# Query and key projections of a two-layer encoder, made with tokens instead of channels on the partitions, in one stream with the Fourier input

## The chip, the cores and the metric

One core of a Trainium2 chip runs the whole program in one launch. The metric is the device time of an execution in microseconds (us). The kernel before took 2951.58 us (median of 3 runs, 2950.15 to 2954.19). TensorE is written PE in the views, its weight loads PEld, VectorE DVE, ScalarE ACT, GpSimd POOL, and SyncE, which issues most DMAs, SP.

## What is computed

Two layers on a residual stream x of 256 tokens by 2048 channels, all in float32. Each has a token mixer, a cross-attention into 256 memory tokens and a gated MLP with a width-3 convolution. The change touches the start of the token mixer:

```python
h = rms_norm(x, mix_pre_g[l])
proj = h @ w_in                       # 2048 x (2048 q + 512 k + 512 v + 1024 fourier)
q = apply_axial_rope(rms_norm(q, q_norm_g), cos, sin)   # 16 heads of 128
k = apply_axial_rope(rms_norm(k, k_norm_g), cos, sin)   # 4 heads of 128
a = blocked_gqa(q, k, v) @ w_attn_o   # softmax attention, 4 q heads to a k head
f = fourier_mix(uf) @ w_four_o        # Re(2-D DFT over positions and channels)
g = sigmoid(h @ w_gate + b_gate)
y = (g[:D] * a + g[D:] * f) @ w_mix_o
```

The rotation takes, in each half of a head, 32 channels x1 and 32 channels x2 to (x1 cos - x2 sin, x2 cos + x1 sin).

## The kernel before

Every float32 product is made of three products of a reduced type: each operand is split into a high and a low part, and high x high, high x low and low x high are summed in PSUM. The activations are split once (A, with channels on the partitions, the high parts of 256 tokens beside their low parts). The weights are split on the fly: a DMA of 512 KB brings 128x1024 floats (w), ScalarE casts them (whi, L133), VectorE subtracts (wlo, L134). Two such pieces are a `Unit` of 1 MB. The pools w, whi and wlo have four buffers each, so a unit is loaded and split while the one before it is multiplied.

There are two ways to multiply. *Weight-stationary* (`ws_chunk`, `block`, L148 to L170): a unit holds the weights of one head's 128 channels for all 16 blocks of input channels; per block one matmul has whi as its stationary operand and streams high and low parts of A (512 columns, L151), a second has wlo and streams the high part (256 columns, L152). The result has channels on the partitions; its two halves are added (`merge`). *Activation-stationary* (`ko_as`, `mm_rows`, L296 to L303): the stationary operand is a 128-token block of A, and 512 columns of weights stream; per input block and token block there are three matmuls of 512 columns. The result has tokens on the partitions. A unit then holds 4 of the 16 input blocks of 512 output columns, and takes 24 matmuls.

A token mixer before the change runs in this order. v, and then the Fourier input in two groups of 512 columns, are made activation-stationary (`ko_as`; the groups are called as). The 20 heads of k and q follow in pairs (`heads`, L608 to L642), weight-stationary: ScalarE squares into hsq, moves 32-partition pieces for the rotation (L600), VectorE rotates with tables over channels (L601 to L606), GpSimd adds squares (L620), and four tiny matmuls per pair sum the squares over partitions (ps_h, L631). The norm of k is spread over the partitions with more small matmuls (ps_kn, L252) and multiplied in. The norm of q is applied later, as the scale of the softmax. Then comes the Fourier stage (`tokens`, `channels`; the matmuls dft and dftx), in which the tiny matmuls of the last pair still stand, and then attention over heads, with the gate projections (g), the Fourier output and the attention output (a) in between.

A tile scheduler sets the order on each engine, and puts in the semaphore waits. Each engine works its own queue in order. At the start of layer 0 SP also loads x once more with tokens on the partitions (X, L558, 2 MB), whose squares (L294) give the norm of the input.

Of the kernel before, what the change touches and what calls it, by code (L numbers as in the profile page):

```python
# [16 lines left out]
P = 128  # L17
# [18 lines left out]
O_BG, O_CW0, O_CW1, O_CW2, O_CB, O_QG, O_KG, NPAR = 112, 144, 232, 320, 408, 496, 497, 498  # L36
# [7 lines left out]
def encoder(ctx: ExitStack, tc: tile.TileContext, t, out):  # L44
# [21 lines left out]
    sides = cp.tile([P, 2], F32, tag="sides", name="sides")  # L66
    nc.vector.memset(sides, 0.0)
    for a in range(2):
        nc.vector.memset(sides[a * 64 : (a + 1) * 64, a : a + 1], 1.0)

# [9 lines left out]
    cos_t = con[:, C_COS : C_COS + T]  # L80
    sin_t = con[:, C_SIN : C_SIN + T]
# [332 lines left out]
    def boundary(y, steps, gains, A, cols, fill=()):  # L414
# [100 lines left out]

    def gains_of(p_, g0):
        return [p_[:, g0 + k : g0 + k + 1] for k in range(KT)]
# [29 lines left out]
    for k in range(KT):  # L547
# [3 lines left out]
        if k == 1:  # L551
            next(feed)
            next(feed)
        if k % 2:
            next(feed)
# [9 lines left out]
    for l in range(L):  # L565
# [5 lines left out]
        k_r = kug[:, 0:4]  # L571
# [3 lines left out]
        def token_major(pss, dst):  # L575
            for j in range(2):
                nc.scalar.activation(dst[:, j], pss[j], AF.Copy, scale=pre.t[:, j : j + 1])

        pss = []
        feed = ko_as(t["w_vu"][l, 1], A, pss)  # L580
        for _ in range(4):
# [6 lines left out]
        for j in range(2):  # L588
            scaled_split(pss_v[j], pre.t[:, j : j + 1], [v[:, j] for v in v_hl])
        run(feed)  # L590
        token_major(pss, u_s[:, :, 0:512])
        pss = []
        run(ko_as(t["w_vu"][l, 2], A, pss))
        token_major(pss, u_s[:, :, 512:1024])

        def rope(raw, g, dst):

            x2 = tmp2("x2")
            for a, b in ((0, 32), (32, 0), (64, 96), (96, 64)):
                nc.scalar.activation(x2[a : a + 32], raw[b : b + 32], AF.Copy, scale=par[b : b + 32, g : g + 1])  # L600
            nc.vector.scalar_tensor_tensor(  # L601
                out=dst, in0=raw, scalar=par[:, g : g + 1], in1=cos_t[:, None, :].to_broadcast([P, 2, T]),
                op0=ALU.mult, op1=ALU.mult,
            )
            nc.vector.tensor_mul(x2, x2, sin_t[:, None, :].to_broadcast([P, 2, T]))
            nc.vector.tensor_add(dst, dst, x2)  # L606

        def heads(w, i, n, g, dst):  # L608

            raw = tmp2("raw")  # L610
            for j in range(2):
                merge(ws_chunk(w[j], A, KT, name="qk"), raw[:, j])
                if j == 0:
                    yield

            sq = tmp2("hsq")
            for a in range(2):
                for b in range(2):
                    nc.scalar.activation(sq[64 * a : 64 * a + 64, b], raw[64 * b : 64 * b + 64, a], AF.Square)
            nc.gpsimd.tensor_add(sq[:, 0], sq[:, 0], sq[:, 1])  # L620
            if dst is None:

                dst = tmp2("q")
                rope(raw, g, dst)
                split(dst, O[:, i : i + 2].rearrange("p h s n -> p s h n"))
            else:
                rope(raw, g, dst)
            yield
            ps = psum_pv("ps_h")
            for j in range(2):  # L630
                nc.tensor.matmul(  # L631
# [611 lines left out]
```

## Time and profile before

| | |
|---|---|
| time, median of 3 runs | 2951.58 us |
| time of the profiled execution | 2949.64 us |
| its span, first to last instruction | 2947.9 us |
| PE busy | 2917.1 us (99%) |
| VectorE, ScalarE, GpSimd busy | 2057.7, 1646.4, 29.6 us |
| DMA | 562.63 MB, mean 191 GB/s |
| granted clock of TensorE | 0.999 of full speed |
| k and q projection, layer 0 | 75.76 to 194.56 us |
| k and q projection, layer 1 | 1545.60 to 1664.75 us |

The first line of the page gives busy time by engine; matmuls are pipelined, so how long a stream of matmuls takes is read from the starts of its instructions in the timeline and not from their durations. The chain of waits (part 4 of the page) tells which engine the end waited for.

### The profile page before, as it was taken

What the parts mean: (1) busy time and instruction counts of PE and PEld (TensorE: products, weight loads), DVE (VectorE), ACT (ScalarE), POOL (GpSimd) and SP (SyncE); (2) the same over time, 40 slices, a digit from 0 to 9 for tenths busy, and PEclk for the clock granted to TensorE, in tenths of its full rate; (3) what the DMA queues carried; (4) which work ended last, traced back from release to release, by engine and by line L of the source; (5) the groups of instructions that cost most, each with busy time, mean ns of one, the idle gap of its engine ahead of it and who ended that gap; (6) DMA issues with size and microseconds to landing.
All of it is one profiled execution on the core that took longest, in us unless ns stands there. A gap on an engine that the chain in (4) does not pass through costs nothing.

```text
span 2947.9 us, 39901 instructions
## 1 busy us (share of the span) xinstructions
PE 2917.1 (99%) x14844; PEld 2464.5 (84%) x14844; DVE 2057.7 (70%) x2963; ACT 1646.4 (56%) x2517; POOL 29.6 (1%) x40
## 2 busy tenths in 40 slices
PE   9999999999999999999999999999999999999998
PEld 7888888887888888888878888888878888888887
DVE  5678766666775767767756786776667757677676
ACT  5776545556554545545547764445565545455454
POOL 0000000000000000000000000000000000000000
PEclk9999999999999999999999999999999999999999
DMA  7554766765456565565645446667554565655655
GB/s 282 166 158 144 233 225 224 226 189 180 163 185 196 186 185 193 183 196 186 214 162 168 143 154 219 220 220 226 189 178 163 182 199 186 187 192 180 199 186 164
DMA packets 162756, 562.63 MB, mean 191 GB/s; under 512 B 18432, under 2 KB 18688, under 8 KB 162432
## 3 DMA queue, kind: packets, MB, share of 16 engines
q1 hardware_dynamic: 160992, 555.61, 58.5%
q0 software_dynamic: 1280, 4.20, 0.4%
q8 instruction: 116, 1.90, 0.3%
q14 instruction: 80, 0.66, 0.1%
q10 hardware_dynamic: 288, 0.27, 0.0%
HBM read 555.81 MB, written 4.19 MB: 190 GB/s over the span
## 4 chain that ended last, share of the span: by engine, by line
PE 92%; DVE 3%; DMA 2%; ACT 2%; issue 1%; SPq 0%; POOL 0%; DVEq 0%; ACTq 0%; POOLq 0%
PE up L151 21%; PE up L152 11%; PE y L303 7%; PE y L302 7%; PE y L301 7%; PE qk L151 4%; PE g L303 4%; PE g L301 4%; PE g L302 4%; PE qk L152 2%; PE a L303 2%; PE a L302 2%; PE a L301 2%; PE as L211 1%; PE as L212 1%; PE as L210 1%
## 5 line engine op out<-in xcount | busy, mean ns | idle before, releaser
L134 DVE TENSOR_TENSOR wlo<-w,whi 128x1024 fp32r<-128x1024 f32 (+1 forms) x989 | 1184.4, 1201 | 667.5 <-ACT whi L133 665.1
L133 ACT CAST whi<-w 128x1024 fp32r<-128x1024 f32 (+1 forms) x989 | 1019.4, 1034 | 1022.2 <-PE up L151 388.1
L151 PE MATMUL up<-A_ff,whi 128*128 128x512 f32 x2688 | 946.2, 397 | 0.0
L152 PE MATMUL up<-A_ff,wlo 128*128 128x256 f32 x2688 | 754.4, 281 | 0.0
L151 PEld LDWEIGHTS up<-A_ff,whi 128*128 128x128 f32 x2688 | 504.6, 188 | 122.4
L152 PEld LDWEIGHTS up<-A_ff,wlo 128*128 128x128 f32 x2688 | 507.8, 189 | 0.3
L302 PE MATMUL y<-wlo,G 128*128 128x512 f32 x704 | 274.1, 389 | 0.8 <-DVE wlo L134 0.8
L301 PE MATMUL y<-whi,G 128*128 128x512 f32 x704 | 274.1, 389 | 0.2 <-ACT whi L133 0.2
L303 PE MATMUL y<-whi,G 128*128 128x512 f32 x704 | 274.0, 389 | 0.0
L151 PE MATMUL qk<-A_mix,whi 128*128 128x512 f32 x640 | 227.2, 398 | 0.0
L303 PE MATMUL g<-whi,A_mix 128*128 128x512 f32 x512 | 201.7, 394 | 0.0
L301 PE MATMUL g<-whi,A_mix 128*128 128x512 f32 x512 | 201.2, 393 | 0.4 <-DVE work L763 0.4
L302 PE MATMUL g<-wlo,A_mix 128*128 128x512 f32 x512 | 200.2, 391 | 0.0
L152 PE MATMUL qk<-A_mix,wlo 128*128 128x256 f32 x640 | 179.3, 280 | 0.0
L302 PEld LDWEIGHTS y<-wlo,G 128*128 128x128 f32 x704 | 132.2, 188 | 28.4 <-DVE wlo L134 1.1
L301 PEld LDWEIGHTS y<-whi,G 128*128 128x128 f32 x704 | 132.1, 188 | 28.0 <-ACT whi L133 0.7
L303 PEld LDWEIGHTS y<-whi,G 128*128 128x128 f32 x704 | 132.1, 188 | 27.6
L151 PEld LDWEIGHTS qk<-A_mix,whi 128*128 128x128 f32 x640 | 120.2, 188 | 27.5
L152 PEld LDWEIGHTS qk<-A_mix,wlo 128*128 128x128 f32 x640 | 120.8, 189 | 0.1
L303 PEld LDWEIGHTS g<-whi,A_mix 128*128 128x128 f32 x512 | 96.2, 188 | 19.2
L301 PEld LDWEIGHTS g<-whi,A_mix 128*128 128x128 f32 x512 | 96.3, 188 | 19.0 <-ACT whi L133 0.8
L302 PEld LDWEIGHTS g<-wlo,A_mix 128*128 128x128 f32 x512 | 96.3, 188 | 18.7
(264 smaller groups left out, 4040.9 us busy)
## 6 DMA issues: line engine op xcount, KB each, us to landing
w<-in_w_up SPq DMA_DIRECT2D x336, 512.0 KB, 3.9
w<-in_w_dn SPq DMA_DIRECT2D x160, 512.0 KB, 3.7
w<-in_w_g SPq DMA_DIRECT2D x128, 512.0 KB, 4.2
w<-in_w_qk SPq DMA_DIRECT2D x80, 512.0 KB, 5.0
w<-in_w_ao SPq DMA_DIRECT2D x64, 512.0 KB, 4.8
w<-in_w_mo SPq DMA_DIRECT2D x64, 512.0 KB, 4.1
w<-in_w_vu SPq DMA_DIRECT2D x47, 512.0 KB, 4.8
w<-in_w_fo SPq DMA_DIRECT2D x32, 512.0 KB, 4.6
```

Source lines behind the costliest of these rows:

```text
L133: nc.scalar.copy(hi[:, :m], w[:, :m])
L134: nc.vector.tensor_sub(lo[:, :m], w[:, :m], hi[:, :m].bitcast(F32))
L151: nc.tensor.matmul(ps, hi, a, start=first, stop=False, skip_group_check=True)
L152: nc.tensor.matmul(ps[:, :T], lo, a[:, 0:T], start=False, stop=last, skip_group_check=True)
L210: nc.tensor.matmul(pss[j], ah, hi, start=kt == 0, stop=False)
L211: nc.tensor.matmul(pss[j], ah, lo, start=False, stop=False)
L212: nc.tensor.matmul(pss[j], al, hi, start=False, stop=kt == KT - 1)
L301: nc.tensor.matmul(ps, ah, hi, start=first, stop=False)
L302: nc.tensor.matmul(ps, ah, lo, start=False, stop=False)
L303: nc.tensor.matmul(ps, al, hi, start=False, stop=last)
```

## The change

- k and q are no longer made weight-stationary. `projected`, which made the gates, is moved up and makes them activation-stationary: five groups of 512 columns (4 heads each), k first, four units a group, 24 matmuls a unit. The two Fourier groups follow in the same stream (`in_columns`, `stream`). The weights lie in DRAM in the other layout, in the same amount.
- The first unit of that stream is prepared earlier: in layer 0 before the last blocks of x are used, in layer 1 in the boundary ahead of the squares of x.
- The norms are summed along the free dimension: for each token block j and head, ScalarE squares 128 columns of PSUM with an accumulated sum (8 per group).
- The rotation reads PSUM on VectorE: one multiplication of 128x512 by a table, two of 128x256 by the other (the halves exchanged by the access pattern), one addition. The gains are multiplied into the tables once per layer (`rotation`, four multiplications of 128x256, behind a broadcast load of 256 KB).
- The result (tokens on partitions) is turned by four transposes per token block and group on TensorE (rt), then split into high and low parts by ScalarE and VectorE, as q and k were before.
- The steps of this work are strewn into the stream by `between`, one per input block.
- Gone: the partition moves, the squares of half heads, GpSimd's additions, ps_h, ps_kn and `merge` of k and q.

```diff
@@ boundary
+        if then is not None:
+            then()
@@ start of layer 0
+        if k == KT - 1:
+            todo, later = in_columns(0)
+            todo[0].make()
@@ new functions
+    def stream(items, between):
+        for i, item in enumerate(items):
+            if i + 1 < len(items):
+                items[i + 1].make()
+            for _ in item.use():
+                between(i)
+                yield
+    def in_columns(l):
+        later = []
+        todo = []
+        for n in range(5):
+            todo += projected(t["w_qk"][l, n], A, "qk", lambda j, ps, row, n=n: later.append((n, j, ps)))
+        for n in range(2):
+            todo += projected(t["w_vu"][l, 1 + n], A, "u", lambda j, ps, row, n=n: later.append((5 + n, j, ps)))
+        return todo, later
@@ the layer
-        pss = []
-        feed = ko_as(t["w_vu"][l, 1], A, pss)
...
+        def rotated(n, j, ps):
...
+            def begin():
+                for h in range(4):
+                    nc.scalar.activation(
+                        unread[:, :P], ps[:, h * P : (h + 1) * P], AF.Square, accum_out=ssq[:, h0 + h, j : j + 1]
+                    )
...
+                nc.vector.tensor_mul(heads[0], heads[1], own[:, None, :].to_broadcast([P, 4, P]))
...
+                for s in range(2):
+                    nc.vector.tensor_mul(
+                        x_[:, :, :, s], p_[:, :, :, 1 - s], o_[:, None, :, s].to_broadcast([P, 4, 2, 32])
+                    )
+            def norm():
+                v = kn[:, :, j]
+                nc.vector.tensor_scalar(v, v, 1.0 / P, pre.et[:, j : j + 1], op0=ALU.mult, op1=ALU.add)
+                rk = rsqrt(v, "kn")
+                nc.vector.tensor_add(x, x, r)
...
+            def add():
+                if n:
+                    nc.vector.tensor_add(r, r, x)
+            def turn():
+                pt = ps_sc.tile([P, 4, P], F32, tag="sc", name="rt")
+                for h in range(4):
+                    nc.tensor.transpose(pt[:, h], r[:, h * P : (h + 1) * P], ident)
...
+                nc.scalar.copy(hi, pt)
+                nc.vector.tensor_sub(lo, pt, hi.bitcast(F32))
+            return [begin, add if n else norm, turn]
+        def between(i):
+            while later:
+                n, j, ps = later.pop(0)
+                if n < 5:
+                    steps.extend(rotated(n, j, ps))
+                else:
+                    c = (n - 5) * 512
+                    nc.scalar.activation(u_s[:, j, c : c + 512], ps, AF.Copy, scale=pre.t[:, j : j + 1])
+            if steps:
+                steps.pop(0)()
+        feed = stream(todo, between)
...
-        def rope(raw, g, dst):
...
-        def heads(w, i, n, g, dst):
...
         ab = [tokens(0)]
-        run(before)
...
-            ss = boundary(y, steps, par[:, O_MIXPRE : O_MIXPRE + KT], A, cols)
+            todo, later = in_columns(l + 1)
+            ss = boundary(y, steps, par[:, O_MIXPRE : O_MIXPRE + KT], A, cols, then=todo[0].make)
```

How the queues stand. TensorE between two heads of a pair before the change (layer 0, first pair of k):

```order
L151 MATMUL qk<-A_mix,whi 128x512
L152 MATMUL qk<-A_mix,wlo 128x256
L631 MATMUL ps_h<-sides,hsq 128x2 [waits Pool_49]
L631 MATMUL ps_h<-sides,hsq 128x2
L151 MATMUL qk<-A_mix,whi 128x512
L152 MATMUL qk<-A_mix,wlo 128x256 [waits DVE_49]
```

TensorE after the change, 23 matmuls into the group that follows the first group of q (psums qk_519 and qk_520 are the finished group's two token blocks, qk_717 and qk_718 the running one's):

```order
L295 MATMUL qk_718<-whi,A_mix 128x512
L296 MATMUL qk_718<-wlo,A_mix 128x512
L671 MATMUL rt<-con,rot 128x128 [waits DVE_49,PE_49]
L671 MATMUL rt<-con,rot 128x128 x3
L297 MATMUL qk_718<-whi,A_mix 128x512
L295 MATMUL qk_717<-whi,A_mix 128x512 [waits Activation_49]
L296 MATMUL qk_717<-wlo,A_mix 128x512
```

The four transposes of the first token block stand there, those of the second 17 matmuls further. In all ten places after a group of q it is so, and after the group of k they stand 36 and another 20 matmuls on.

VectorE after the change, around the end of that same group:

```order
L128 TENSOR_TENSOR wlo<-w_705,whi 128x1024 [waits DMAHW1_49,Activation_49]
L128 TENSOR_TENSOR wlo<-w_707,whi 128x1024 [waits DMAHW2_49,Activation_49]
L648 TENSOR_TENSOR rot<-qk_519,kug 128x512 [waits Activation_49]
L652 TENSOR_TENSOR x_726<-qk_519,kug 128x8x32 x2
L648 TENSOR_TENSOR rot<-qk_520,kug 128x512 [waits PE_49,Activation_49]
L666 TENSOR_TENSOR rot<-rot,x_726 128x512 [waits DVE_49]
L652 TENSOR_TENSOR x_728<-qk_520,kug 128x8x32 x2
L128 TENSOR_TENSOR wlo<-w_769,whi 128x1024 [waits DMAHW3_49,Activation_49]
```

ScalarE beside it, where the squares of each psum are made:

```order
L127 CAST whi<-w_705 128x1024 [waits DMAHW1_49,DVE_49,PE_49]
L644 ACTIVATE unread,qs<-qk_519 128x128 [waits PE_49]
L644 ACTIVATE unread,qs<-qk_519 128x128 [waits Activation_49]
L127 CAST whi<-w_707 128x1024 [waits DMAHW2_49,DVE_49,PE_49]
L644 ACTIVATE unread,qs<-qk_519 128x128 [waits Activation_49] x2
L644 ACTIVATE unread,qs<-qk_520 128x128 [waits Activation_49] x4
L127 CAST whi<-w_769 128x1024 [waits DMAHW3_49,DVE_49,PE_49]
```

VectorE's product with a psum waits for ScalarE's squares of that psum, and the transposes wait for VectorE's addition (L666).

ScalarE at the end of v in layer 0, before the change (w_325 is the first piece of the Fourier weights, which are multiplied next):

```order
L133 CAST whi<-w_247 128x1024 [waits DMAHW7_49,DVE_49,PE_49]
L294 ACTIVATE unread,ss_pre<-X 128x512 [waits DMAHW2_49]
L294 ACTIVATE unread,ss_pre<-X 128x512 [waits Activation_49] x3
L133 CAST whi<-w_325 128x1024 [waits DMAHW4_49,DVE_49,PE_49]
L294 ACTIVATE unread,ss_pre<-X 128x512 [waits Activation_49]
```

And after it (w_289 and w_291 are the first unit of the stream, w_335 begins the second):

```order
L127 CAST whi<-w_243 128x1024 [waits DMAHW7_49,DVE_49,PE_49]
L127 CAST whi<-w_289 128x1024 [waits DMAHW0_49,DVE_49,PE_49]
L127 CAST whi<-w_291 128x1024 [waits DMAHW1_49,DVE_49,PE_49]
L288 ACTIVATE unread,ss_pre<-X 128x512 [waits DMAHW4_49]
L288 ACTIVATE unread,ss_pre<-X 128x512 [waits Activation_49] x3
L127 CAST whi<-w_335 128x1024 [waits DMAHW6_49,DVE_49,PE_49]
```

The casts of the unit that TensorE needs next now stand ahead of the squares that wait for X.

## Rows read from the trace of the kernel before

**Rows 1.** The page: busy time by engine, and the chain that ended last, as shares of the span by engine.

```profile
PE 2917.1 (99%) x14844; PEld 2464.5 (84%) x14844; DVE 2057.7 (70%) x2963; ACT 1646.4 (56%) x2517; POOL 29.6 (1%) x40
...
PE 92%; DVE 3%; DMA 2%; ACT 2%; issue 1%; SPq 0%; POOL 0%; DVEq 0%; ACTq 0%; POOLq 0%
```

**Rows 2.** Groups of instructions by line: the 512-column matmuls of k and q of both layers (count, busy us, mean ns).

```profile
L151 PE MATMUL qk<-A_mix,whi 128*128 128x512 f32 x640 | 227.2, 398 | 0.0
```

**Rows 3.** Timeline of PE (start us, duration us): the first matmul of the k and q projection in each layer, its 39th weight block, and the first matmul of the Fourier stage behind it.

```profile
75.76 0.39 PE L151 MATMUL qk<-A_mix,whi 128*128 128x512 f32 x1
...
89.17 0.40 PE L151 MATMUL qk<-A_mix,whi 128*128 128x512 f32 x1
...
194.56 2.32 PE L684 MATMUL dft<-w,kug 128*128 128x256 f32 x10
...
1545.60 0.39 PE L151 MATMUL qk<-A_mix,whi 128*128 128x512 f32 x1
...
1664.75 2.32 PE L684 MATMUL dft<-w,kug 128*128 128x256 f32 x10
```

**Rows 4.** Timeline of PE in the Fourier input of layer 0, activation-stationary: the first and the last of 113 matmuls that follow each other.

```profile
50.15 0.39 PE L211 MATMUL as<-wlo,A_mix 128*128 128x512 f32 x1
...
75.53 0.39 PE L212 MATMUL as<-whi,A_mix 128*128 128x512 f32 x1
```

**Rows 5.** Timeline of PE around eight transposes (mt) in a stream of 512-column matmuls.

```profile
315.37 0.40 PE L302 MATMUL g<-wlo,A_mix 128*128 128x512 f32 x1
315.61 1.12 PE L848 MATMUL mt<-con,work 128*128 128x128 f32 x8
316.49 0.48 PE L303 MATMUL g<-whi,A_mix 128*128 128x512 f32 x1
316.80 0.39 PE L301 MATMUL g<-whi,A_mix 128*128 128x512 f32 x1
```

**Rows 6.** Groups of instructions by line on ScalarE and VectorE: what the new steps resemble (count, busy us, mean ns, idle before).

```profile
L223 ACT COPY half<-qk 128x256 f32<-128x256 f32 x40 | 14.7, 367 | 3.2 <-PE qk L152 2.9
L691 ACT COPY ab<-dft 128x512 f32<-128x512 f32 x8 | 4.5, 588 | 1.6 <-PE dft L684 1.6
L134 DVE TENSOR_TENSOR wlo<-w,whi 128x1024 fp32r<-128x1024 f32 x947 | 1155.5, 1223 | 642.8 <-ACT whi L133 640.6
L409 DVE TENSOR_TENSOR a<-xt,par 128x512 f32<-128x512 f32 x40 | 26.0, 683 | 5.1 <-PE xt L407 5.1
L224 DVE TENSOR_TENSOR raw<-qk,half 128x256 f32<-128x256 f32 x40 | 16.7, 419 | 1.1 <-ACT half L223 1.1
```

**Rows 7.** Timeline of VectorE: two operations of 128x512 back to back, as one row.

```profile
313.54 1.28 DVE L844 SCALAR_TENSOR_TENSOR work<-work,a 128x512 f32<-128x512 f32 x2
```

**Rows 8.** Timeline of SP, ScalarE and VectorE at the start of layer 0: the issue of X's load, squares of 512 columns and the cast between them, and the low part behind it (the idle time before a row, and what ended it, in brackets).

```profile
16.52 0.43 SPq L558 DMA_DIRECT2D X<-in_xt  x1
...
27.32 0.63 ACT L294 ACTIVATE unread<-X 128x512 bf16<-128x512 f32 x1 [5.82 <-DMA X<-in_xt]
...
28.07 0.63 ACT L294 ACTIVATE unread<-X 128x512 bf16<-128x512 f32 x1
...
30.21 1.03 ACT L133 CAST whi<-w 128x1024 fp32r<-128x1024 f32 x1
31.15 0.63 ACT L294 ACTIVATE unread<-X 128x512 bf16<-128x512 f32 x1
31.27 1.23 DVE L134 TENSOR_TENSOR wlo<-w,whi 128x1024 fp32r<-128x1024 f32 x1 [8.38 <-ACT whi L133]
```

**Rows 9.** Timeline of PE in the Fourier stages of both layers: the last norm sums, and the Fourier matmuls that follow.

```profile
197.36 0.61 PE L631 MATMUL ps_h<-sides,hsq 128*128 128x2 f32 x4 [0.49 <-POOL hsq L620]
197.83 1.54 PE L684 MATMUL dft<-w,kug 128*128 128x256 f32 x6
...
1667.64 0.61 PE L631 MATMUL ps_h<-sides,hsq 128*128 128x2 f32 x4 [0.56 <-POOL hsq L620]
1668.10 1.54 PE L684 MATMUL dft<-w,kug 128*128 128x256 f32 x6
```

**Rows 10.** Timeline of PE at the start of layer 0, where v ends and the Fourier input begins.

```profile
29.88 0.39 PE L212 MATMUL as<-whi,A_mix 128*128 128x512 f32 x1
31.30 0.73 PE L210 MATMUL as<-whi,A_mix 128*128 128x512 f32 x2 [1.03 <-ACT whi L133]
32.56 0.50 PE L211 MATMUL as<-wlo,A_mix 128*128 128x512 f32 x1 [0.53 <-DVE wlo L134]
```

**Rows 11.** Stretches of 10 us in layer 0: X's load in flight, and the Fourier input (length, busy us of PE, PEld, DVE, ACT, POOL with counts, granted clock, DMA share, GB/s).

```profile
20.00:30.00 10.00, 10.00 (x46) 8.17 (x44) 2.89 (x4) 4.09 (x9) 0.00 (x0) 1.00 0.97 391
...
60.00:70.00 10.00, 10.00 (x46) 8.29 (x45) 4.79 (x4) 3.86 (x4) 0.00 (x0) 1.00 0.62 206
```

**Rows 12.** Timeline of PE: the first turned softmax of attention in both layers.

```profile
213.22 0.33 PE L499 MATMUL pt<-con,e 128*128 128x128 f32 x1 [0.84 <-DVE e L491]
...
1683.75 0.33 PE L499 MATMUL pt<-con,e 128*128 128x128 f32 x1 [1.08 <-DVE e L491]
```

More of the change, by code (lines that the diff above doesn't have):

```diff
@@ L412, in renew, with boundary @@
         nc.vector.tensor_sub(lo, a, hi.bitcast(F32))
-    def boundary(y, steps, gains, A, cols, fill=()):
+    def boundary(y, steps, gains, A, cols, fill=(), then=None):
         fill = list(fill)
@@ L514, in att_out, with projected, __init__, make @@
         nc.vector.tensor_sub(o[:, h, 1], pv[:, :T], o[:, h, 0].bitcast(F32))
+    def projected(src, S, name, finish, first=None):
+        class Item:
+            pss = []
+            def __init__(self, u):
+                self.u = u
+            def make(self):
+                if self.u == 0 and first is not None:
+                    Item.row = first()
+                self.w = unit(src[self.u])
+            def use(self):
+                if self.u == 0:
+                    Item.pss = [psum(f"{name}{j}") for j in range(2)]
+                for k in range(4):
+                    kt = 4 * self.u + k
+                    for j in range(2):
+                        mm_rows(Item.pss[j], S, kt, j, self.w, k * 512, kt == 0, kt == KT - 1)
+                    yield
+                if self.u == 3:
+                    for j in range(2):
+                        finish(j, Item.pss[j], getattr(Item, "row", None))
+        return [Item(u) for u in range(4)]
+    def stream(items, between):
[4 more added lines that the diff above has]
+                between(i)
+                yield
+    def in_columns(l):
[6 more added lines that the diff above has]
+        return todo, later
     def gains_of(p_, g0):
@@ L582, in encoder @@
+        def between(i):
[9 more added lines that the diff above has]
+        feed = stream(todo, between)
+        for _ in range(3):
             next(feed)
@@ L608, in heads @@
-        def heads(w, i, n, g, dst):
[L610 to L631, printed above, removed]
-                    ps[:, 2 * j : 2 * j + 2], sq[:, 0, j * P : (j + 1) * P], sides, start=True, stop=True
-                )
-            nc.vector.scalar_tensor_tensor(
-                out=n[:, i : i + 2],
-                in0=ps[:, 0:4].rearrange("p (j a) -> p a j", a=2),
-                scalar=1.0 / P,
-                in1=pre.et[:, None, :].to_broadcast([P, 2, 2]),
-                op0=ALU.mult,
-                op1=ALU.add,
-            )
@@ L644, in encoder @@
[L644 to L664 removed]
+        between(None)
@@ L1221, in _layout @@
     a["par"] = par
+    partner = np.arange(P) ^ 32
+    a["rope_g"] = np.stack(
+        [np.concatenate([g[l][o] for g in (i["q_norm_g"], i["k_norm_g"]) for o in (slice(None), partner)]) for l in range(L)]
+    )
     for k, v in st.items():
```

123 lines of the change are left out of this document (43 added, 80 removed).

## The prediction

> **What bounds the kernel now.** I read the page first: TensorE is busy 99% of the span and holds 92% of the chain that ended last [rows 1]. So an edit is worth what it takes from TensorE's queue, or what it saves or adds in waits there; ScalarE, VectorE and GpSimd count only where TensorE waits for them. A busy share cannot show how long a stream of matmuls takes, so I went on to the timeline of TensorE and read starts. The sum below is made against the profiled execution, 2949.6 us, which is 1.9 us under the median of the runs, 2951.58.
>
> **The matmuls of k and q.** Before, the projection runs from 75.76 to 194.56 us in layer 0 and from 1545.60 to 1664.75 in layer 1 [rows 3]: 118.80 + 119.15 = 237.95 us, the small norm matmuls and their waits included. It holds 640 pairs of a 512- and a 256-column matmul [rows 2], and 38 pairs take 89.17 - 75.76 = 13.41 us [rows 3], 0.353 us a pair of 768 columns. After, the same columns go in matmuls of 512 only: 5 groups x 16 input blocks x 6 = 480 a layer, 960 in all. That form is in the trace, with the same operands: in the Fourier input 112 matmuls take 75.53 - 50.15 = 25.38 us, 0.2266 us each [rows 4]. 960 x 0.2266 = 217.5 us. The columns are equal; what falls is the number of matmuls, 1280 to 960, and each has a share that does not depend on its columns.
>
> The Trainium skill (TensorE: Matmul & The Clock Gate, Back-to-back issue gap) gives an isolated gap of N/2.4 + 2.5 ns at full clock. By that a pair would take 325 ns and a 512-column matmul 216 ns, 207.9 us against 207.2, and the change would win next to nothing here; the rows above show a larger fixed share, and the sum goes by them.
>
> **The transposes.** New on TensorE are 20 times four transposes (two token blocks x five groups x two layers). Eight of the kind, mt, hold the stream from 315.61 to 316.49, and the matmul behind them takes 0.31 us to the next start where 0.2266 is usual [rows 5]. Four then cost 0.44 + 0.085 = 0.525 us, 20 cost 10.5. The projection gains 237.95 - 217.5 - 10.5 = 9.9 us.
>
> **The waits in front of the transposes.** This is the step that before does not show, and it decides. Let G be the end of issue of a group's last matmul. The transposes of the first token block stand 23 matmuls on, at G + 5.21 us (23 x 0.2266). Ahead of them lies a chain. The first block's psum is complete about 0.5 us before G (its last matmul starts four matmuls before G and lasts 0.39 us), the second's at G + 0.16. ScalarE makes two squares, the cast that stands between them, two squares, then the four of the second block. A square of 512 columns with its accumulated sum repeats every 0.75 us (27.32 to 28.07), a cast of 1024 holds ScalarE 0.94 us (30.21 to 31.15) [rows 8]. No 128-column square is in the trace: 256 columns fewer take 588 - 367 = 221 ns less [rows 6], so 384 fewer take about 0.33 less, and I take 0.42 us, an estimate from these rows. Then the first four squares are done at G + 2.2, all eight at G + 3.9. VectorE has the low part of that cast until about G + 2.6 (1.34, when the cast ends, plus 1.22 [rows 6]); then the first product, 0.60 (two such take 1.28 [rows 7], one alone 0.68), two of 256 columns, 0.34 each (0.42 less the same overlap [rows 6]): G + 3.9; the second block's product to 4.5, the addition with its 0.68 to 5.2. The chain ends where TensorE arrives. The second block's transposes, 17 matmuls later, stand behind a low part, a split of the first block and another low part; added up from the same rows these end within 0.2 us of their place. After the group of k the norm with its small steps adds some 3 us, and there the transposes stand 36 matmuls on (8.16 us). I take 1.5 us of waits in all, 0.075 a time. Bounds: nothing, if squares are cheaper; 27 us, if a square takes as long as one of 512 columns. I stay near the low end, because a square this narrow is nearer to the 256-column copy (367 ns) plus its sum than to 0.75.
>
> What is queued behind a late chain: on VectorE the low parts of weights that are needed 5 to 11 us later, so it costs its own wait and no more.
>
> The Trainium skill (PSUM — Partial Sum Buffer, PSUM bank collisions raise a hardware error) says that two engines, ScalarE and VectorE reads included, may not use one bank and quadrant at once and have to be kept apart by waits. It speaks against this change: four squares must pass before VectorE may start, and the sum without that rule would be the same less the 1.5 us. The order of the changed kernel has that wait; no row of before shows two engines at one bank.
>
> **The norm sums in the Fourier stage** go: there TensorE waits 0.49 and 0.56 us for GpSimd and then spends 0.47 and 0.46 us until the next Fourier matmul [rows 9]. Gain 2.0 us. The earlier ones are within the stage's time above.
>
> **The start of layer 0.** After v ends, at 29.88 + 0.23 = 30.11, TensorE gets its next matmuls at 31.30 and 32.56 [rows 10]; in a full stream the one at 32.56 would start at 30.56. The loss is 2.0 us, and the cause is order: the cast it waits for stands behind four squares, which wait until 27.32 for X [rows 8]. After, the first unit is cast ahead of them. X's load is issued behind 1 MB more; at 391 GB/s [rows 11] it lands 2.7 us later, at 30.0. Four squares make it 33.0, the cast of the second unit's first piece 33.95, its low part 35.2 (1.23 us). TensorE wants it at 30.11 + 24 x 0.2266 = 35.55. So the wait goes, 2.0 us, and X's load is late next, with 0.35 us to spare. Bounds: -1 (X another microsecond and more late) to +2.0. In layer 1 no wait is there to win.
>
> **At nothing.** Tables: four products of 256 columns a layer, 0.42 us each, on VectorE, which is less than half busy in such a stream (4.79 of 10 us [rows 11]); without that cover they would cost 1.7 us a layer. The stream's weights come at 1 MB in 24 x 0.2266 = 5.44 us, 193 GB/s, under the 206 of the Fourier input with TensorE at 10.00 of 10 us [rows 11]. The Fourier stage now follows the last Fourier columns at once, but its first two steps use columns copied 20 us before, and the two copies of the last group (some 0.59 us each [rows 6]) lie beside them. The first softmax waits 0.84 and 1.08 us now [rows 12]; its scores now come behind the Fourier stage instead of within it, its chain starts later and has more work ahead of it: I count 0, bounds -1 to +1 a layer.
>
> **Sum.** -9.9 - 2.0 - 2.0 + 1.5 = -12.4 us: 2937.2 on the profiled execution, 2939.2 against the median.
>
> **Rivals.** (All on the median's footing.)
> 1. *Small waits.* The chain is 0.8 us longer than worked out, ten groups, 8 us instead of 1.5: 2945.7. For it: it ends just where TensorE arrives. Against: mt, placed by the same scheduler, stands without a wait [rows 5]. 0.16.
> 2. *The squares make it slower.* Place: the chain in front of each group's first transposes. Each square over 0.42 us shifts the chain eight times, 80 times in all. At 0.59 us the gain is gone, 80 x 0.17 = 13.9. At 0.75, the row of 512 columns, it is 26.4 us: 2951.58 - 13.9 + 26.4 = 2964.1. For it: each square carries a second instruction for its sum and waits for the one before; against: the narrower rows. 0.08.
> 3. *A column costs what a column costs.* If 512 columns took 512/768 of a pair, 0.2353 us, 960 take 225.9, the projection gains 1.5, and all 4.0: 2947.6. It is the page's case, in rows of this trace; [rows 4] speak against it outright. 0.04. The change would then not do what it does by count.
> 4. *X's load late*, waits at the start of layer 0 remain: 2941 to 2942, within the forecast's range.
>
> **Chances.** Forecast 0.67, rival 1 0.16, rival 2 0.08, rival 3 0.04, and 0.05 for something else (attention woven otherwise, say). A measurement of this kernel can tell some 0.2%, 5.9 us, from no change. Faster by more: the forecast, and half of rival 1, 0.75. Same: the other half and rival 3 and some of the rest, 0.15. Slower: rival 2 and the rest, 0.10. Range: no waits and a shorter first softmax give 2951.58 - 13.9 - 2 = 2935.7, less 2 for the runs' own spread, 2933.5; upwards rivals 1 and 3, 2948.
>
> **What would show it.** In the profile after: k and q about 114 us a layer from the first qk matmul to the first of the Fourier columns (108.8 + 5.25), 0.2266 us from start to start; waits in front of rt below 2 us in total; no wait behind v at 30 us; no GpSimd wait in the Fourier stage. I am wrong if rt waits for the addition by more than half a microsecond each time (squares over 0.5 us), or if the stream itself runs slower than the Fourier input of before.

## The result, and the profile after

The changed kernel takes 2934.51 us (median of 4 runs, 2933.39 to 2936.53); the kernel before took 2950.86 on the same chip. The ratio is 0.9943, with a 95% interval of 0.9926 to 0.996: 16 us less, between 12 and 22. A second measurement gave 2935.74 us (2932.01 to 2937.02) and 0.9934, 0.9921 to 0.9948. The forecast was 2939.2 and faster; it was faster by some 4 us more. Two of the experiments below had one execution each that took two or more times as long, and their medians leave it out. The profiled executions are 2949.64 and 2934.76 us, spans 2947.9 and 2932.7, and the ledger below is made between these two.

The page of after, busy time and the chain that ended last, as in [rows 1]:

```profile
PE 2908.9 (99%) x14492; PEld 2447.2 (83%) x14492; DVE 2041.8 (70%) x2926; ACT 1574.2 (54%) x2479; POOL 14.2 (0%) x20
...
PE 94%; DMA 2%; DVE 2%; ACT 1%; issue 1%; SPq 0%; DVEq 0%; ACTq 0%
```

TensorE bounds it as before. Its busy time fell by 8.2 us only; the rest came out of waits. The waits of PE in after (whom for, us in total, times, longest):

```profile
PE as L297 <- DVE A_ff L406: 4.2, 4, 1.7
PE as L295 <- ACT A_mix L405: 2.2, 1, 2.2
...
PE g L295 <- DVE work L775: 0.2, 1, 0.2
```

Neither rt nor qk nor pt stands there: no transposes of k and q wait, and the waits of [rows 9], [rows 10] and [rows 12] are gone. The timeline of PE in after: where v ends, a set of transposes, the starts of the Fourier columns (u) and the Fourier stage (dft), and the first turned softmax; then the same of layer 1.

```profile
29.74 0.39 PE L206 MATMUL as<-whi,A_mix 128*128 128x512 f32 x1
29.96 0.39 PE L295 MATMUL qk<-whi,A_mix 128*128 128x512 f32 x1
...
35.40 0.61 PE L295 MATMUL qk<-whi,A_mix 128*128 128x512 f32 x2
36.04 0.50 PE L296 MATMUL qk<-wlo,A_mix 128*128 128x512 f32 x1
36.38 0.39 PE L297 MATMUL qk<-whi,A_mix 128*128 128x512 f32 x1
...
80.01 0.60 PE L671 MATMUL rt<-con,rot 128*128 128x128 f32 x4
80.36 0.48 PE L297 MATMUL qk<-whi,A_mix 128*128 128x512 f32 x1
80.68 0.40 PE L295 MATMUL qk<-whi,A_mix 128*128 128x512 f32 x1
...
142.99 0.39 PE L295 MATMUL u<-whi,A_mix 128*128 128x512 f32 x1
...
187.49 3.61 PE L722 MATMUL dft<-w,kug 128*128 128x256 f32 x16
...
205.34 0.27 PE L495 MATMUL pt<-con,e 128*128 128x128 f32 x1
...
1494.02 0.39 PE L295 MATMUL qk<-whi,A_mix 128*128 128x512 f32 x1
...
1606.70 0.39 PE L295 MATMUL u<-whi,A_mix 128*128 128x512 f32 x1
...
1651.19 1.02 PE L722 MATMUL dft<-w,kug 128*128 128x256 f32 x4
```

From the end of v to the Fourier stage, k, q and both Fourier groups take 187.49 - 29.97 = 157.52 us in layer 0, where before took 194.56 - 30.11 = 164.45; in layer 1 157.17 (1494.02 to 1651.19) against 162.67 (1502.08 to 1664.75): 12.4 us together. The stages between, by the starts of their first matmul on PE:

| stage, ends with the start of | before, us | after, us | difference |
|---|---|---|---|
| Fourier stage, layer 0 | 194.56 | 187.49 | -7.07 |
| output projection y of the mixer | 340.44 | 336.44 | -4.00 |
| y of the cross-attention | 166.13 | 166.35 | +0.22 |
| first up of the MLP | 56.23 | 58.32 | +2.09 |
| boundary to layer 1 (as of A_mix) | 717.96 | 717.58 | -0.38 |
| Fourier stage, layer 1 | 189.43 | 185.01 | -4.42 |
| y of the mixer | 338.52 | 335.41 | -3.11 |
| y of the cross-attention | 166.24 | 166.22 | -0.02 |
| first up of the MLP | 56.26 | 57.41 | +1.15 |
| the end's matmuls | 713.42 | 713.40 | -0.02 |

The gain is made in the mixer of each layer, as forecast, and some of it is given back at three boundaries that the change does not touch. There the granted clock (column behind POOL's) differs. Windows of 8 us from the first matmul of each boundary's projection (towards the MLP, layer 0; to layer 1; towards the MLP, layer 1), first of before, then of after:

```profile
729.44:737.44 8.00, 6.82 (x32) 5.29 (x32) 8.00 (x14) 7.78 (x21) 0.00 (x0) 1.00 0.53 175
1475.32:1483.32 8.00, 7.37 (x36) 5.69 (x36) 7.96 (x14) 5.60 (x17) 0.00 (x0) 1.00 0.16 39
2197.86:2205.86 8.00, 6.87 (x32) 5.28 (x32) 8.00 (x14) 7.78 (x21) 0.00 (x0) 1.00 0.52 177
```

```profile
718.80:726.80 8.00, 6.27 (x19) 4.71 (x20) 8.00 (x13) 7.39 (x20) 0.00 (x0) 0.79 0.64 185
1466.18:1474.18 8.00, 8.00 (x32) 6.28 (x32) 6.68 (x12) 5.62 (x16) 0.00 (x0) 0.79 0.12 37
2180.74:2188.74 8.00, 6.58 (x21) 4.97 (x22) 8.00 (x13) 7.62 (x20) 0.00 (x0) 0.79 0.56 176
```

In each of after's, seven or eight matmuls of 512 columns follow each other by 0.427 us in place of 0.2266 (the lower of the clock's two levels, 1.2 GHz), which costs 1.4 to 1.6 us. Just ahead TensorE had stood idle for 1.73, 2.18 and 1.42 us (part of the first two rows of the waits).

### The profile page after: what moved, and what is told of

Read it like the earlier page. It is cut to its first block, busy times and chain, and to the rows that moved or that the text cites. A ratio compares the mean times of both kernels' runs of the same rounds, so it can differ in the third digit from the quotient of the medians.

```text
span 2932.7 us, 39086 instructions
## 1 busy us (share of the span) xinstructions
PE 2908.9 (99%) x14492; PEld 2447.2 (83%) x14492; DVE 2041.8 (70%) x2926; ACT 1574.2 (54%) x2479; POOL 14.2 (0%) x20
## 4 chain that ended last, share of the span: by engine, by line
PE 94%; DMA 2%; DVE 2%; ACT 1%; issue 1%; SPq 0%; DVEq 0%; ACTq 0%
PE up L145 21%; PE up L146 11%; PE y L295 7%; PE y L296 7%; PE y L297 7%; PE g L295 4%; PE g L296 4%; PE g L297 4%; PE qk L296 2%; PE qk L297 2%; PE qk L295 2%; PE a L297 2%; PE a L295 2%; PE a L296 2%; PE as L297 1%; PE as L295 1%
## 5 line engine op out<-in xcount | busy, mean ns | idle before, releaser
L297 PE MATMUL qk<-whi,A_mix 128*128 128x512 f32 x320 | 125.4, 392 | 0.0
L296 PE MATMUL qk<-wlo,A_mix 128*128 128x512 f32 x320 | 125.4, 392 | 0.0
L295 PE MATMUL qk<-whi,A_mix 128*128 128x512 f32 x320 | 124.7, 390 | 0.0
L1029 ACT ACTIVATE cv<-u,par 128x256 f32<-128x256 f32 x176 | 105.2, 598 | 7.6 <-DVE u L1027 7.6
```

What stands on the lines that cost most here:

```text
L295: nc.tensor.matmul(ps, ah, hi, start=first, stop=False)
L296: nc.tensor.matmul(ps, ah, lo, start=False, stop=False)
L297: nc.tensor.matmul(ps, al, hi, start=False, stop=last)
L1029: nc.scalar.activation(r, u, AF.Identity, scale=par[:, O_CW1 + c : O_CW1 + c + 1], bias=par[:, O_CB + c : O_CB + c + 1])
```

## The experiments

My theory after the result had four parts: the shorter stream comes from fewer and equal matmuls; the start from the early cast; the missing waits of the attention from the order of the stream; the give-back from the clock, which falls where TensorE has been idle. Each run below has its rival in its expectation. The runs were made on three chips, each beside runs of the kernel before; where two times are close, the ratios to those runs are the fairer comparison (after: 0.9943, and 0.9934 the second time).

**Halves of the matmuls.** In the groups of k and q, `mm_rows` is replaced:

```diff
-        nc.tensor.matmul(ps, ah, hi, start=first, stop=False)
-        nc.tensor.matmul(ps, ah, lo, start=False, stop=False)
-        nc.tensor.matmul(ps, al, hi, start=False, stop=last)
+        for c in (0, T):
+            for i, (x, y) in enumerate(((ah, hi), (ah, lo), (al, hi))):
+                nc.tensor.matmul(ps[:, c : c + T], x, y[:, c : c + T], start=first and i == 0, stop=last and i == 2, ...)
```

> Each matmul of 512 columns of q and k is made as two of 256, with the same stationary block and the same columns in all (480 matmuls a layer become 960). Theory of the prediction, a share per matmul beside its columns: in the rows of before the pair of 512 and 256 columns took 353 ns and the 512 alone takes 226.6 ns, so 256 columns cost 126.4 ns and each split costs 2 x 126.4 - 226.6 = 26 ns: + 12.6 us in each q/k stage, + 25 us in all, about 2960 us. Rival, a column costs what a column costs: 0, about 2934.5 us, and the gain of the change came from elsewhere.

(The two halves of each sum start apart here, so this kernel's q and k are not the right ones; only its time is read.) Measured 2948.69 us, + 14.2, and 0.999 of the kernel before (0.998 to 1.0001): little is left of the change's gain. The stage up to Fourier grows by 7.4 and 5.5 us (the second would be 7.1 without the fall of the clock in after); from the first to the last qk matmul it is 6.9 and 6.5 us (112.80 to 119.67, 112.45 to 118.97), 0.4 of that a wait. Its timeline of PE:

```profile
50.04 0.28 PE L306 MATMUL qk<-wlo,A_mix 128*128 128x256 f32 x1
50.16 0.40 PE L306 MATMUL qk<-whi,A_mix 128*128 128x256 f32 x2
50.40 0.28 PE L306 MATMUL qk<-wlo,A_mix 128*128 128x256 f32 x1
```

256 columns take 0.120 us, 512 take 0.2266. So a column takes 0.4164 ns and each matmul 13.4 ns beside its columns; a split costs that once, 960 x 13.4 ns = 12.9 us, and the two stretches grew by 13.0 beside the wait. "A column costs what a column costs" is refuted. My 26 ns was wrong by half: I had got the 256 columns by subtracting 226.6 from the pair's 353, and so put down to the short matmul what belongs to the pair.

**By turns or grouped, in the kernel before.** The 16 matmuls of 512 columns of a chunk first, then its 16 of 256:

```diff
+        for k in range(nkt):
+            nc.tensor.matmul(ps, w(k * P)[0], flat(A, k), start=k == 0, stop=False, ...)
+        for k in range(nkt):
+            nc.tensor.matmul(ps[:, :T], w(k * P)[1], flat(A, k)[:, 0:T], start=False, stop=k == nkt - 1, ...)
...
-                merge(ws_chunk(w[j], A, KT, name="qk"), raw[:, j])
+                merge(ws_grouped(w[j], A, KT, "qk"), raw[:, j])
```

> The kernel before, with the 16 matmuls of 512 columns of a q or k chunk first and its 16 of 256 columns behind them, in place of by turns (640 pairs in all). By turns a pair takes 353 ns there (0.233 us from a 512 to the 256 behind it, 0.120 from the 256 to the next 512), while halves of 256 alone took 0.120 and 512 alone 0.2266 us: 346.6 ns. Theory: the rest, 6.4 ns a pair, is the price of two lengths by turns: 640 x 15/16 x 6.4 ns = - 3.8 us, some 1.9 in each q/k stage, about 2947.5. Rival: it belongs to this kind of matmul (A stationary's place taken by weights), whatever its neighbours: 0.

Measured 2950.37 us, ratio to before 0.9991 (0.9982 to 1.0), against a before of 2952.89. The timeline of PE:

```profile
75.52 3.79 PE L167 MATMUL qk<-A_mix,whi 128*128 128x512 f32 x16
...
96.31 2.08 PE L169 MATMUL qk<-A_mix,wlo 128*128 128x256 f32 x16
98.23 3.82 PE L167 MATMUL qk<-A_mix,whi 128*128 128x512 f32 x16
101.88 2.08 PE L169 MATMUL qk<-A_mix,wlo 128*128 128x256 f32 x16
...
192.96 2.75 PE L695 MATMUL dft<-w,kug 128*128 128x256 f32 x12
```

16 of 256 take 1.92 us and 16 of 512 take 3.65, 5.57 us a chunk or 348 ns a pair, against 353 by turns: within a chunk the turns cost some 5 ns a pair, 1.5 us a layer. From the first qk matmul to the first dft the stages are shorter by 1.4 and 1.7 us (118.80 and 119.15 to 117.44 each); but 0.64 of each is a wait in front of ps_kn that before has and this run has not, so 0.7 and 1.1 are left for the matmuls. By the medians alone the interval touches no change. So of the 8.4 us that the matmuls themselves gave (225.9 to 217.5), 320 fewer matmuls explain 320 x 13.4 ns = 4.3, the turns 1.8 to 3.1, and 1.0 to 2.3 stay open (the rival, something in this kind of matmul, may have them).

**The cast at its old place.**

```diff
             todo, later = in_columns(0)
-            todo[0].make()
...
-            ss = boundary(y, steps, ..., A, cols, then=todo[0].make)
+            ss = boundary(y, steps, ..., A, cols)
...
+        todo[0].make()
         feed = stream(todo, between)
```

> The first unit of the stream is cast where the stream begins, behind the squares of X, in both layers, as before; all else as after. Theory: TensorE waits again behind v in layer 0, for some 1.0 us on the cast and 0.5 us on the low part, and the small wait at 35.4 us goes: + 1.0 to + 2.0 us, about 2936; in layer 1, where before showed no wait there, 0. Rival, the squares were not what the start waited for (the load of the weights was): no wait behind v, 0, about 2934.5.

Measured 2936.01 us, + 1.5, and 0.9943 of the kernel before (0.9927 to 0.9958), as after. Its timeline of PE has both waits again:

```profile
30.09 0.39 PE L206 MATMUL as<-whi,A_mix 128*128 128x512 f32 x1
31.90 0.73 PE L295 MATMUL qk<-whi,A_mix 128*128 128x512 f32 x2 [1.42 <-ACT whi L127]
33.16 0.50 PE L296 MATMUL qk<-wlo,A_mix 128*128 128x512 f32 x1 [0.53 <-DVE wlo L128]
```

In layer 1 no row appears. From the end of v to the Fourier stage it takes 159.64 us (30.32 to 189.96) where after takes 157.52: the early cast is worth 2.1 us, by the wait. The medians do not show it: their spread is 3.6 us, and this run's mixer has a wait of 1.9 us (g, for work) where after has 0.2.

**The Fourier columns first.**

```diff
-        for n in range(5): todo += projected(t["w_qk"][l, n], ...)
         for n in range(2): todo += projected(t["w_vu"][l, 1 + n], ...)
+        for n in range(5): todo += projected(t["w_qk"][l, n], ...)
...
         ab = [tokens(0)]
+        between(None)
         for g in range(1, 4):
             ab.append(tokens(g))
+            between(None)
             channels(g - 1, ab[g - 1], px)
+            between(None)
```

> The Fourier columns come first in the stream and k and q behind them, so that the last block of q is rotated and transposed among the Fourier matmuls; the qs factors follow those squares. All else as after. Theory: the 1.9 us by which the first transposes of the softmax waited before (0.84 and 1.08) went because the Fourier columns now stand between the last q and the attention; so here they come back, 0.8 to 1.5 us a layer, and the transposes of the last q block wait in the Fourier stage for 0 to 1.5 us a layer: + 1.6 to + 6 us, about 2938. Rival: those waits went with the norm sums (their matmuls, their addition on GpSimd and the vector work behind them), so the order does nothing: within 0.6 us of 2934.5.

Measured 2937.03 us, + 2.5, but 0.9945 of the kernel before (0.9931 to 0.996), which is after's ratio: the time shows no difference, and only the trace can be read. Among its waits of PE:

```profile
PE rt L671 <- DVE rot L666: 1.5, 2, 0.8
```

The last block's transposes wait 0.75 us a layer in the Fourier stage, so the order is worth that. But no wait of pt comes back: on this half the theory falls. What the trace of before shows at that place is VectorE's queue: the division of the first softmax (ri) stands behind a sum of Fourier weights (sd), and that one waits for its load.

```profile
211.16 0.69 DVE L782 TENSOR_TENSOR sd<-w 128x512 f32<-128x512 f32 x1 [1.07 <-DMA w<-in_w_fo]
...
212.16 0.15 DVE L489 RECIPROCAL ri<-su 128x2 f32<-128x2 f32 x1
```

In layer 1 sd waits 1.30 us there. In after and in this run the scheduler puts both sums behind the first maximum of the scores, and there is no wait for that load. The grouped kernel above bears this out: it has before's stream and its norm sums, but there the division stands ahead of sd, and although sd still waits for its load (0.28 us, in layer 1 0.85), the first turned softmax does not wait in either layer.

```profile
209.55 0.17 DVE L500 RECIPROCAL ri<-su 128x2 f32<-128x2 f32 x1 [0.20 <-ACT e L496]
...
210.99 0.69 DVE L793 TENSOR_TENSOR sd<-w 128x512 f32<-128x512 f32 x1 [0.28 <-DMA w<-in_w_fo]
```

So neither the order of the stream nor the end of the norm sums is needed for this gain; where the scheduler puts sd goes with it in each of these runs. No run moves sd alone.

**Each square twice.**

```diff
                 for h in range(4):
-                    nc.scalar.activation(unread[:, :P], ps[...], AF.Square, accum_out=ssq[...])
+                    for _ in range(2):
+                        nc.scalar.activation(unread[:, :P], ps[...], AF.Square, accum_out=ssq[...])
```

> Each square of q and k is taken twice (the second writes the same sum again): 80 more on ScalarE at the 0.40 us from start to start that after shows, 32 us of ScalarE's time. Theory of the chain: rt of a q block starts 0.25 us after its rotated rows are done (79.76 and 80.01 us), and the cast between the squares comes 0.8 to 1.6 us later, with the low part and the rotation behind it on VectorE: 0.5 to 1.4 us in front of rt at 10 groups, + 5 to + 14 us, about 2944. Rival: the rotation does not wait for the squares and the casts are a unit ahead, ScalarE being idle for nearly half of the stage: 0, within 1 us of 2934.5.

Measured 2935.29 us, + 0.8, and 0.9939 of the kernel before (0.9921 to 0.9957): the rival's figure, but not for its reason. Its timelines of VectorE and PE, at the group whose transposes stand at 80.01 in after:

```profile
78.52 0.69 DVE L649 TENSOR_TENSOR rot<-qk,kug 128x512 f32<-128x512 f32 x1 [1.03 <-ACT unread L645]
```

```profile
81.76 0.63 PE L672 MATMUL rt<-con,rot 128*128 128x128 f32 x4
```

The rotation does wait for the squares, 1.03 us, and the chain is later by what I expected. TensorE does not feel it, because its order was made again: the scheduler puts rt behind 29 matmuls of the next group in place of 23, and the second block's behind 51 in place of 40. Only k's first block waits, once in each layer, 0.4 us in all; the first blocks of q wait 0.04 us each.

**The memory rows' place.**

```diff
-            yield from stream(items, beside)
+            for i, item in enumerate(items):
+                if i + 1 < len(items):
+                    items[i + 1].make()
+                yield from item.use()
+                beside(i)
```

> After, with the norm of the memory rows (layer 0) taken behind the last matmuls of an item as before, in place of within it. Theory: the wait of 1.09 us that before showed in front of the transposes mt near 463 us came from those loads and squares standing where the gate's vector work was due, and comes back: + 1 us, a row 'mt <- work' of about 1.1 us. Rival: the wait went because the stage now begins at another phase of its loads: no such row, 0.

One run, 2931.7 us, and in its whole mixer stage of layer 0 a single wait of PE:

```profile
PE g L295 <- DVE work L775: 0.5, 1, 0.5
```

No mt: the theory falls. The wait for mt (the transposes of the memory rows) comes and goes among the runs (1.2 us with the Fourier columns first, 0.4 with the late cast, none in after and its repetition) and is not this change's.

**Kept busy at the boundaries.** Matmuls of ones into an unused bank:

```diff
+            keep_busy(4 if then is not None else 1)
-            cols.block(0, 0)
+            cols.block(0, 0, 0 if then is not None else 3)
```

> After, with a few matmuls of ones into an unused bank in the boundaries' waits (each about 0.42 us in the rows of the start: 1 and 3 of them at the FFN boundaries, 4 at the boundary to layer 1); no data waits for them. Theory: the clock fell in after's three boundaries (0.81, 0.84, 0.84; spacing of 512 columns 0.427 in place of 0.2266 us over some 8 matmuls) because TensorE had been idle just before; kept busy, it stays 1.00: - 1.6 us at each, up to - 4.8, about 2930; the head of each boundary is not later. Rival: the clock falls there for another reason: the stretch stays at 0.81 to 0.84, 0 to + 1 us.

Measured 2933.23 us (2932.41 to 2933.41, 5 runs). The three windows:

```profile
720.36:728.36 8.00, 6.49 (x30) 5.30 (x31) 8.00 (x13) 7.39 (x20) 0.00 (x0) 1.00 0.55 172
1466.47:1474.47 8.00, 7.37 (x36) 5.69 (x36) 7.99 (x14) 5.60 (x17) 0.00 (x0) 1.00 0.12 37
2180.85:2188.85 8.00, 7.00 (x36) 5.65 (x34) 8.00 (x14) 7.78 (x21) 0.00 (x0) 1.00 0.58 173
```

The clock stays at 1.00. But TensorE was not kept busy at the two FFN boundaries: the two rows of ones that stand in the wait take 0.39 us, the others were ordered ahead of it, and waits of 1.51 and 1.00 us remain.

```profile
720.93 0.39 PE L303 MATMUL idle<-ones 128*128 128x128 f32 x2
722.82 0.50 PE L326 MATMUL as<-home,A_ff 128*128 128x512 f32 x1 [1.51 <-DVE A_ff L418]
```

Behind such waits the clock fell in some executions and not in others (next run), so this one execution does not tell the theory from its rival. The three stages concerned are 57.11, 183.88 and 56.01 us, 3.7 less than in after, of which the profiled time kept 1.4 (other waits of the mixer were 2.3 longer); by the medians 1.3 us less, within the runs' spread.

**The changed kernel again.**

> The changed kernel once more, for the spread of its time and for the three boundaries. If the fall of the granted clock there is decided anew in each execution, the profile may show fewer than three stretches at half clock, and a stage without one is 1.2 to 2 us shorter (from OX to up 56.2 in place of 58.3 us); the median stays at 2934.5 within 1.5 us. If the fall belongs to this kernel's order of work, all three are there again.

2935.74 us. Two of its three windows fell, the third did not:

```profile
721.17:729.17 8.00, 6.27 (x19) 4.75 (x20) 8.00 (x13) 7.38 (x20) 0.00 (x0) 0.79 0.59 170
1469.27:1477.27 8.00, 7.71 (x27) 5.84 (x28) 6.74 (x11) 5.59 (x16) 0.00 (x0) 0.79 0.13 36
2184.73:2192.73 8.00, 6.89 (x32) 5.28 (x32) 8.00 (x12) 7.78 (x21) 0.00 (x0) 1.00 0.57 176
```

So the fall is decided in each execution. Over the nine profiled executions with this boundary code (before, the grouped one, after twice, and five of the runs above) there are 27 such windows, and 11 fell (7 to 14 matmuls); the longest wait there was 1.21 to 2.86 us where they fell, and 1.04 to 2.06 where they did not, so its length alone does not decide. The grouped kernel, with before's order, fell at the boundary to layer 1, so the fall does not need the change. Whether the change makes it more frequent is not shown: it fell in one of six windows with before's order and in ten of 21 with after's.

**Low halves last, in both kernels.** In a block of four input blocks, the eight matmuls on A's high half ahead of the four on its low half:

```diff
-                mm_rows(self.ps[j], self.A, k, j, self.w[g], i * 512, k == 0, k == KT - 1)
+                todo += [(0, ah, hi), (0, ah, lo), (1, al, hi)]
+            todo.sort(key=lambda x: x[0])
+            for i, (_, a, b) in enumerate(todo):
+                nc.tensor.matmul(self.ps[j], a, b, start=g + i == 0, stop=g == 3 and i == 11)
```

> After, but in each block of four of the boundary's projection the matmuls on the low half of A come behind the eight on its high half. Theory: at the start of the two FFN boundaries TensorE does not wait 1.73 and 1.42 us for the low half of A_ff, and its granted clock stays 1.00 there where after shows 0.81 and 0.84; VectorE's chain (8.6 of 9.2 us busy there) gives part of it back: 1.3 to 3.8 us each; in the boundary to layer 1 the wait of 2.18 us is for the high half and stays: - 3 to - 8 us, likely - 5, about 2929.5. Rival: the boundary's end is set by VectorE's and ScalarE's chain, whatever TensorE does at its head: 0 to - 1 us.

> The same edit in the kernel before. There the granted clock in these boundaries is 1.00 and VectorE has no gap in them, so by the theory only a part of the waits (1.17 and 0.51, 1.13 and 0.51 us) goes: 0 to - 3.3 us, likely - 1.5, about 2949. If the clock's fall in after's boundaries took some 1.6 us each of the gain, this kernel's distance to the other one with low halves last is larger than that of after to before by 2 to 5 us (18 to 21 in place of 16); if the clock has nothing to do with it, the two distances are the same.

On after: 2926.1 us (2925.11 to 2928.81), ratio to before 0.9911 (0.9898 to 0.9925). On before: 2945.0, 0.9974 (0.9965 to 0.9983). The edit makes both kernels faster. On before it gave 8.7 us by the medians, where I had expected 3.3 at most: the profiled executions differ by 6.0, about 3.4 of it in the two stages to the first up and 1.1 in the boundary to layer 1; the rest I cannot name. Its windows on after:

```profile
718.72:726.72 8.00, 7.51 (x36) 5.70 (x36) 7.92 (x14) 7.55 (x20) 0.00 (x0) 1.00 0.61 174
1461.80:1469.80 8.00, 7.23 (x37) 5.78 (x37) 8.00 (x14) 5.60 (x17) 0.00 (x0) 1.00 0.16 37
2175.33:2183.33 8.00, 7.65 (x39) 6.09 (x40) 7.86 (x12) 7.81 (x21) 0.00 (x0) 1.00 0.54 174
```

The stages to the first up are 54.13 and 53.95 us. In the nine executions without the edit they are 56.1 to 58.5 us in the 12 cases without a fall (median 56.4) and 57.4 to 59.7 in the six with one (median 58.1): 2.4 us less than without a fall, and another 1.7 less than with one. The rival (VectorE's chain gives it all back) is refuted. Whether the clock took a share of the change's gain, these two do not settle: they lie 18.9 us apart, after and before 16.4 and 17.2, all within the intervals.

With three matmuls of ones at the boundary to layer 1 as well:

> The low halves last in the boundary's projection, and three matmuls of ones while TensorE waits at the boundary to layer 1, for the high half of A_mix (wait 1.3 us in the run with low halves last, 2.2 in after). Theory: nothing falls to half clock, and the time is that of the run with low halves last, 2926 within 1.5 us, with a smaller spread than its 3.7 us. Rival: ones in front of the first block put it off, + 0.4 to + 1.3 us.

2926.53 us (2925.18 to 2927.77): nothing more. Of the 12 windows in the four kernels with low halves last or ones, none fell, where 11 of 27 did otherwise. If all 39 windows were alike, that would come about by chance about once in 130 times, so TensorE's idle time ahead very likely plays a part. It is not shown: in some of the 12 the wait was as long as before (1.32 us twice, 1.51 once), and what else decides is open. The Trainium skill (TensorE: Matmul & The Clock Gate, What's actually happening) says that the same kernel's count of slow matmuls differs from run to run, at a kernel's start; the windows of this case, with 7 to 14 slow matmuls or none, agree in the middle of the program.

## Why the prediction was right, and where it was off

**The matmuls.** As worked out: 0.2266 us each from start to start, 113.0 us (142.99 - 29.96) and 112.7 us (1606.70 - 1494.02) from the first qk to the first u, where I had 114. The last two sets of transposes fall behind that mark, which I had not seen; over the whole stream ten sets take at most 157.17 - 672 x 0.2266 = 4.9 us, 0.49 each (0.44 by the rows of the set at 80.01) against 0.525. The prediction gave the gain to the number of matmuls, and that is a part only. Of its 237.95 - 217.5 = 20.4 us the pairs gave 8.4, and the other 12.0 are the norm matmuls among them: by their starts ps_h and ps_kn take 9.8 us of the two stages and the wait in front of ps_kn 1.3. So the transposes, 9.8 us in all, take back about what the norm matmuls gave, and the net, some 10.6 us, is mostly the pairs'. Within that 8.4, why the count matters was half right: a share of 13.4 ns per matmul explains 4.3, two lengths by turns 1.8 to 3.1. The Trainium skill (TensorE: Matmul & The Clock Gate, Back-to-back issue gap) has 2.5 ns in place of the 13.4; here the rows decide.

**The waits in front of rt.** The chain was read rightly and its term a little too high: 1.5 us of a possible 27, and it is nothing. The width of a square was right (0.42 us; the rows give 0.40, 74.31 to 74.71):

```profile
74.31 0.28 ACT L644 ACTIVATE unread<-qk 128x128 bf16<-128x128 f32 x1 [0.98 <-PE qk L297]
74.48 0.19 ACT L644 ACTIVATION_READ_ACCUMULATOR unread<-qk 128x1 f32 x1
74.71 0.28 ACT L644 ACTIVATE unread<-qk 128x128 bf16<-128x128 f32 x1
```

```profile
79.08 0.68 DVE L666 TENSOR_TENSOR rot<-rot,x 128x512 f32<-128x512 f32 x1
```

The chain ends at 79.76, TensorE arrives at 80.01; at the other groups of q, too, 0.25 us are to spare. But the bound of 27 us was wrong in kind: I held the place of rt in TensorE's queue fixed, and with squares twice as many the scheduler moved it. "The squares make it slower" could therefore hardly happen. The wait of VectorE for the squares (1.03 us with each square twice) agrees with the Trainium skill (PSUM — Partial Sum Buffer, PSUM bank collisions raise a hardware error): two readers of one bank are kept apart. No run here lets them read at once.

**The norm sums in the Fourier stage** went with what they cost [rows 9], 2.0 us; no row of PE waits for GpSimd.

**The start.** 1.7 of the 2.0 us: v is followed at once, and X's load is late next, as forecast. It landed near 30.8 us, not 30.0, and the second unit's low part is 0.30 us late (35.40 to 36.38 takes 0.98 us where 0.68 is usual). X is first read here:

```profile
30.80 0.63 ACT L288 ACTIVATE unread<-X 128x512 bf16<-128x512 f32 x1 [4.68 <-DMA X<-in_xt]
```

**At nothing** failed at one place, at the edge of its bounds: the first softmax no longer waits, 1.9 us in both layers. I had expected its chain to have more work ahead of it; it has less, since the load that VectorE waited for is not in its way. This is luck: the same happened in the grouped kernel, by the scheduler's order alone.

**Sum.** Stream and start -12.4 (forecast -10.4), norm sums -2.0, first softmax -1.9, mt and g in layer 0 -1.3; some 0.9 us a layer between Fourier stage and y I cannot name; the boundaries give back about 4. That is 15.2 on the profiled execution, where I had 12.4. The terms that I worked out came to 14.4 for 12.4; the terms that I had not forecast are 5.0 us of gain and 4 of loss, and it is luck that they nearly cancel. The measured 2934.51 lies below the 2935.7 that my lower bound was added up from; it lies in the stated range by the 2 us that this allowed for the spread of the runs. What I left out altogether, the clock at the boundaries, is as large as the terms that I worked out to a tenth. The profiled execution of before has no fall and that of after three, so this ledger charges all of it to the change; how much of it is in each kernel's median is open. Slips that change nothing: 80 x 0.17 is 13.6 and not 13.9, 640 x 325 ns is 208.0 and not 207.9 us, and the places after a group of q, where the transposes stand 23 and 40 matmuls on, are eight and not ten.

## What to carry to other kernels

Price a stream by its starts: columns, plus a share for each matmul, and price a form by a stream of that form, not by subtraction from a mixed one. Where a scheduler makes the order, a longer chain moves its consumer too, so bound a new wait by what the order can no longer cover, not by a fixed place. Look at the granted clock at boundaries where the main engine idles (here 1.2 to 2.9 us), and give it there the work whose operands come first.

## What the runs showed of the hardware

TensorE, back to back with new stationary blocks at full clock: 512 columns 226.6 ns, 256 columns 120 ns; 512 and 256 by turns 353 ns a pair, grouped 348. Four transposes of 128x128 put into a stream of 512 columns lengthen it by 0.44 to 0.49 us. A square of 128x128 with its accumulated sum repeats every 0.40 us on ScalarE, 276 ns and a second instruction of 194. Behind waits of 1.21 to 2.86 us the granted clock fell to the lower level for 7 to 14 matmuls in 11 of 27 windows, in some executions of a kernel and not in others, and in none of 12 where that idle time was mostly shortened.
